# Two of the first layer's down products, for the second token half, and the first norm as work of the delta rule mixer's own order

## The chip, the cores and the metric

The kernel runs on one core of one Trainium2 chip. TensorE (PE) multiplies matrices into PSUM; VectorE (DVE), ScalarE (ACT) and GpSimd (POOL) do elementwise work; SyncE's queue (SP) issues nearly all transfers. The metric is the device time of one execution in microseconds (us), the median of several runs.

## What is computed

A trunk of two layers over 1024 tokens of width 1024, in float32. Layer 0 mixes tokens by gated linear attention, layer 1 by the gated delta rule; behind each mixer stands a dense feed-forward block, and a norm stands at the end:

```python
for i in range(DEPTH):
    hn = rms_norm(h, mix_norm_w[i])
    h = h + (gla_mixer(hn, ...) if i % 2 == 0 else gdn_mixer(hn, ...))
    h = h + swiglu(rms_norm(h, ffn_norm_w[i]), ffn_w_gate_up[i], ffn_w_down[i])
return rms_norm(h, final_norm_w)

def swiglu(h, w_gate_up, w_down):
    gate, up = jnp.split(h @ w_gate_up, 2, axis=-1)
    return (jax.nn.silu(gate) * up) @ w_down
```

What is changed is the last product of layer 0 (activations of 1024 x 2816 times `w_down`, 2816 x 1024, added to `h`) and the beginning of `gdn_mixer` in layer 1.

## The kernel before

Every large product keeps float32 accuracy with three matmuls: each operand is split into a rounded part `hi` (a cast on ACT) and the rest `lo` (a subtraction), and `hi*hi`, `hi*lo` and `lo*hi` are added in PSUM. The residual `h` stays on chip as 8 token tiles of 128 rows; a token half is 4 of them.

**The down products (`downs`).** The product is cut 2 x 2 x 2 (tokens in halves, 2816 in even and odd k-tiles, 1024 columns in halves) and computed by seven products of sums instead of eight. Each of the seven runs over 11 k-tiles in 6 groups (one of 1, five of 2) with 4 token tiles: 132 matmuls of 128x512. Three loops hold two products each in step, a fourth holds one; PSUM banks `pa` collect four of the products and are added to a place of `h` after each, `pc` is used for the other three. The activations come from DRAM (`act`), the weights from the input; loads and sums go through tiles `ra*`, `rb*` of two buffers, the sums `sk`, `tk` stay. Operands are split by ACT and DVE into three slots per tag.

**The mixer (`gdn`).** It opens its own pools: `wraw` (tag `raw`, two slots) for what is loaded, `wsplit` (tags `whi` and `wlo`, two slots each) for the split, made by `loadw` with ACT for `whi` and POOL for `wlo`. The first norm (`norm(0)`) runs ahead of everything, then a written-out order: strands (`seq`, `post`, `join`, `prep`, `inputs`, `solve`, one unit after another, 16 units) go on whenever their event or due time on a virtual clock has come, and `dense` (projections `keys`, `values`, `late`, and the output product `out`) fills PE in between. PE keeps this order; the other engines and SP are ordered by a planner that simulates. A unit's `solve` is a chain of 31 steps of two DVE instructions, with transfers before and after it; `join`, `seq` and `post` follow. `values(1)` waits until `seq(0)` has turned its values, `keys(3)` until `seq(0)` has passed, `values(2)` for `seq(1)`. The part of the code that stands at the mixer's start is:

```python
for _ in norm(0):
    pass
with self.tc.manual_schedule(engines={mybir.EngineType.PE}):
    O.run([each(seq), each(post), each(join), each(prep), inputs(), each(solve)], dense())
```

`addout` multiplies two k-tiles of an output product for each token tile and adds the result to `h` on DVE. `lowproj` is the narrow projection that the gates need; it takes slots of `raw` and `whi` as well.

Of the kernel before, what the change touches and what calls it, by code (L numbers as in the profile page):

```python
# [22 lines left out]
P = 128  # L23
D = 1024
# [71 lines left out]
class Trunk:  # L96
# [63 lines left out]
    def loadw(self, srcs, shape):  # L160

        nc = self.nc
        raw = self.wr.tile(shape, F32, name="raw", tag="raw")
        hi = self.ws.tile(shape, F32R, name="whi", tag="whi")
        lo = self.ws.tile(shape, F32R, name="wlo", tag="wlo")
        for sl, src in srcs:
            nc.sync.dma_start(raw[:, :, sl], src)
        nc.scalar.copy(hi, raw)  # L168

        n = shape[1] // 4 or 1  # L170
        for k in range(0, shape[1], n):
            sl = slice(k, k + n)
            if shape[2] * n > 256:
                for c in range(0, shape[2], 256):
                    cs = slice(c, c + 256)
                    nc.gpsimd.tensor_tensor(out=lo[:, sl, cs], in0=raw[:, sl, cs], in1=hi[:, sl, cs].bitcast(F32),  # L176
                                            op=ALU.subtract)
            else:
                nc.gpsimd.tensor_tensor(out=lo[:, sl], in0=raw[:, sl], in1=hi[:, sl].bitcast(F32), op=ALU.subtract)  # L179
        return hi, lo  # L180

    def loadcols(self, w, cols):

# [132 lines left out]

    def addout(self, half, w, lhs, cc):

        for t in range(C):
            ps = self.dps()  # L320
            for k in range(2):
                self.mm3(ps, [v[:, t * P:(t + 1) * P] for v in lhs[k]],
                         [v[:, k, :] for v in w], k == 0, k == 1)
                yield
            o = self.h[:, half * C + t, cc * 512:(cc + 1) * 512]
            self.nc.vector.tensor_tensor(out=o, in0=o, in1=ps, op=ALU.add)  # L326

    def loadrows(self, w, r0, cc):

# [9 lines left out]

    def outparts(self, half, w, r0, oT):  # L340
        for cc in range(2):
            yield from self.addout(half, self.loadrows(w, r0, cc), oT, cc)

    def outproj(self, *args):
        for _ in self.outparts(*args):
# [243 lines left out]
    def gdn(self):  # L589
# [5 lines left out]
        with ExitStack() as es:  # L595
# [22 lines left out]

            def gates(x, half):

                pl = self.lowproj(w_in, 6 * D, B, x)
                low = mx.tile([2 * B, HT], F32, name="low", tag="raw", bufs=2)
                S.copy(low, pl[0:2 * B, :])
                yield 2.0
# [49 lines left out]
            keyed, valued, scored, solved, joined, turned, passed, posted, gating = (events() for _ in range(9))  # L674
            gated = [Event(), Event()]
            gts = [None, None]
            U = [{} for _ in range(UN)]
            x = []

# [36 lines left out]
            def values(n):  # L716
                if n < UN:
                    if n:
                        yield turned[n - 1]
                    for i in range(2):  # L720
                        yield from conv(16 + 2 * (n % NQ) + i, f"v{i}", n, valued if i else None)
# [22 lines left out]

            def inputs():

                yield from gates(x, 0)
                yield free[1]
                yield from norm(1)
                O.set(ready[1], 1.0)  # L750
                yield from gates(x, 1)
                yield free[2]
                yield from self.normparts(self.head, 0, self.ffnw[1], self.xp, mx, "raw")
                O.set(ready[2], 1.0)

            def dense():
                yield from keys(0)
                yield from values(0)
                yield from late(0)
                yield from keys(1)  # L760
                yield from late(1)
                yield from keys(2)
                yield from values(1)
                for m in range(1, UN):
                    if m + 2 in (NQ, UN):
                        yield from values(m + 1)
                        yield from late(m + 1)
                        O.set(free[1 if m + 2 == NQ else 2])
                        yield from out(m - 1)
                        if m + 2 == NQ:  # L770
                            yield ready[1]
                            yield from keys(NQ)
                    else:
                        yield from keys(m + 2)
                        yield from out(m - 1)
                        yield from values(m + 1)
                        yield from late(m + 1)
                yield ready[2]
                yield from self.headparts(1, mx, ("v", "v", "raw"))
                yield from out(UN - 1)  # L780
# [276 lines left out]
            def each(f):  # L1057
                for n in range(UN):
                    yield from f(n)
            for _ in norm(0):  # L1060
                pass
            with self.tc.manual_schedule(engines={mybir.EngineType.PE}):
                O.run([each(seq), each(post), each(join), each(prep), inputs(), each(solve)], dense())

# [46 lines left out]
    def ffn(self, l):  # L1111
        with ExitStack() as es:
            xo = self.pool(es, "xops", 1)
            B = dict(b11=[t[:, 0:4] for t in self.head], b21=[t[:, 4:8] for t in self.head])
            for n in ("t1", "t2", "b22", "t3", "t4"):
                B[n] = [xo.tile([P, 4, HT], F32R, name=f"{n}{h}", tag=f"{n}{h}") for h in ("hi", "lo")]
            self.inputsums(l, B)
            self.gateups(l, B)
        self.xs.__exit__(None, None, None)
        self.downs(self.a["ffn_w_down"][l], self.act)  # L1120

    def pool(self, es, name, bufs, **kw):
        return es.enter_context(self.tc.tile_pool(name=name, bufs=bufs, reuse_waits="tile", **kw))
# [124 lines left out]
                V.tensor_tensor(out=p1, in0=p1, in1=pa, op=ALU.mult)  # L1248
                nc.sync.dma_start(self.act[f][:, 0:HT], p1)

    def downs(self, w, act):

# [5 lines left out]
        with ExitStack() as es:  # L1260
# [26 lines left out]
            def product(g, x, y, pss, first, outs):  # L1287
# [3 lines left out]
                for t in range(C):  # L1291
                    self.prod(pss[t], [v[:, :, t * P:(t + 1) * P] for v in x], y, first and g[0] == 0)
                    if g is groups[-1]:
                        for th, ch in outs:
                            o = self.h[:, th * C + t, ch * HT:(ch + 1) * HT]
                            V.tensor_tensor(out=o, in0=o, in1=pss[t], op=ALU.add)

            banks = lambda own: [own() for _ in range(3)] + [self.prepps()]
            of = lambda t, g: t[:, g[0]:g[0] + g[1]]
            pa, pc = banks(self.dps), banks(self.seqps)  # L1300
            for g in groups:
                b11, a11 = b(g, 0, 0), a(g, 0, 0)
                product(g, a11, b11, pa, True, [(0, 0)])
                b12, a21, a22 = b(g, 0, 1), a(g, 0, 1), a(g, 1, 1)
                s1, t1 = of(sk, g), of(tk, g)
                sum_(s1, a21, a22, ALU.add)
                sum_(t1, b12, b11)
                product(g, s1, t1, pc, True, [(1, 1), (0, 1)])
            pc = banks(self.seqps)
            for g in groups:  # L1310

                a11, b22 = a(g, 0, 0), b(g, 1, 1)
                s, t = of(sk, g), of(tk, g)
                sum_(s, s, a11)
                sum_(t, b22, t)
                product(g, s, t, pa, False, [(0, 1)])
                a12, b21 = a(g, 1, 0), b(g, 1, 0)
                product(g, a12, b21, pc, True, [(0, 0)])
                sum_(s, a12, s)
            pc = banks(self.seqps)  # L1320
            for g in groups:
                a11, a21, b12, b22 = a(g, 0, 0), a(g, 0, 1), b(g, 0, 1), b(g, 1, 1)
                sum_(a11, a11, a21)
                sum_(b12, b22, b12)
                product(g, a11, b12, pa, False, [(1, 1)])
                product(g, of(sk, g), b22, pc, True, [(0, 1)])
# [87 lines left out]
```

## Time and profile before

| | us |
|---|---|
| median of 3 runs | 3215.63 (3211.54 to 3217.33) |
| profiled execution | 3215.21 |
| its span, first to last instruction | 3213.4 |
| mean granted TensorE clock | 0.965 |
| down products of layer 0, PE | 1031.1 to 1243.5 |
| first projection of the mixer | 1261.83 |

Times inside the profile count from the span's first instruction. Busy times of engines overlap. A matmul's duration includes its way through the array; what counts for a row of matmuls is the distance between their starts.

### The profile page before, as it was taken

How to read it: one execution, taken by the hardware profiler on the slowest of the kernel's cores; microseconds unless marked ns; L12 is line 12 of the kernel's file. 1: busy time of each engine (PE TensorE's matmuls, PEld its weight loads, DVE VectorE, ACT ScalarE, POOL GpSimd, SP SyncE). 2: the span in 40 equal slices, each digit the busy share in tenths (PEclk: the TensorE clock that was granted, in tenths of full speed). 3: DMA queues.
4: the chain of work that ended last, by engine and by line, in shares of the span. 5: the costliest groups of instructions: out<-in, count | busy, mean ns of one | idle time of the engine just before them, and what ended most of it. 6: DMA issues, size and time to landing. Idle time of an engine off the chain costs nothing.

```text
span 3213.4 us, 41887 instructions
## 1 busy us (share of the span) xinstructions
PE 2948.6 (92%) x14547; PEld 2433.6 (76%) x14547; DVE 1968.8 (61%) x4228; ACT 1410.4 (44%) x2581; POOL 1300.5 (40%) x1561
## 2 busy tenths in 40 slices
PE   6999999899999998879999987999999889999998
PEld 5877777678887887667777776777777668888786
DVE  5364665633223875777777868778778543332786
ACT  5354454433433334435444453554544433333333
POOL 5454654545553002613443444344444445555001
PEclk9999999999999999889999998999999899999999
DMA  4222222332223842312222212222232232221862
GB/s 127 73 61 66 66 61 69 94 106 79 89 82 115 287 144 67 86 32 72 70 73 66 66 54 72 61 71 71 65 79 63 86 112 79 86 79 60 293 221 92
DMA packets 386882, 296.83 MB, mean 92 GB/s; under 512 B 70087, under 2 KB 312206, under 8 KB 386670
## 3 DMA queue, kind: packets, MB, share of 16 engines
q1 hardware_dynamic: 386606, 294.15, 30.4%
q8 instruction: 114, 1.87, 0.2%
q14 instruction: 98, 0.80, 0.1%
q0 software_dynamic: 64, 0.02, 0.0%
HBM read 259.49 MB, written 34.60 MB: 92 GB/s over the span
## 4 chain that ended last, share of the span: by engine, by line
PE 64%; DVE 24%; DMA 4%; issue 3%; ACT 3%; POOL 2%; SPq 1%; DVEq 0%; POOLq 0%; ACTq 0%
PE pd L211 38%; PE pq L211 14%; PE pp L211 8%; DVE xix L896 4%; DVE tmpx L894 4%; DVE v L702 1%; DMA nbx<-d 1%; POOL wlo L179 1%; PE pp L494 1%; DVE k L702 1%; DVE h L326 1%; PE pp L217 1%; DMA rb<-in_ffn_w_down_dram 1%; DVE st L496 1%; DMA p<-part 1%
## 5 line engine op out<-in xcount | busy, mean ns | idle before, releaser
L179 POOL TENSOR_TENSOR wlo<-raw,whi 128x256 fp32r<-128x256 f32 x624 | 473.9, 789 | 463.5 <-ACT whi L168 424.4
L211 PE MATMUL pd<-xhi,whi 128*128 128x512 f32 x1072 | 448.0, 418 | 0.8 <-ACT part L1093 0.7
L211 PE MATMUL pd<-xhi,wlo 128*128 128x512 f32 x1072 | 426.1, 397 | 0.0
L211 PE MATMUL pd<-xlo,whi 128*128 128x512 f32 x1072 | 424.9, 396 | 0.0
L168 ACT CAST whi<-raw 128x1024 fp32r<-128x1024 f32 x204 | 213.8, 1049 | 247.2 <-PE pd L211 140.7
L1129 POOL TENSOR_TENSOR olo<-s,ohi 128x512 fp32r<-128x512 f32 x152 | 195.9, 1290 | 205.9 <-ACT ohi L1128 205.9
L1129 POOL TENSOR_TENSOR olo<-raw,ohi 128x512 fp32r<-128x512 f32 x138 | 190.8, 1385 | 202.8 <-ACT ohi L1128 178.3
L211 PEld LDWEIGHTS pd<-xhi,wlo 128*128 128x128 f32 x1072 | 204.4, 191 | 46.1 <-POOL wlo L179 0.5
L176 POOL TENSOR_TENSOR wlo<-raw,whi 128x256 fp32r<-128x256 f32 x192 | 146.5, 792 | 217.9 <-ACT whi L168 200.0
L211 PEld LDWEIGHTS pd<-xhi,whi 128*128 128x128 f32 x1072 | 205.3, 192 | 38.4 <-ACT part L1093 1.7
L211 PEld LDWEIGHTS pd<-xlo,whi 128*128 128x128 f32 x1072 | 205.6, 192 | 36.7 <-issue 0.3
L1128 ACT CAST ohi<-s 128x512 fp32r<-128x512 f32 x152 | 94.3, 622 | 230.6 <-PE pd L211 174.0
L211 PE MATMUL pd<-whi,ohi 128*128 128x512 f32 x384 | 165.9, 432 | 11.9 <-ACT q L700 8.7
L894 DVE TENSOR_TENSOR tmpx<-nbx,xix 128x60 f32<-128x60 f32 (+24 forms) x496 | 152.0, 307 | 35.9 <-DMA nbx<-d 23.2
L1128 ACT CAST ohi<-raw 128x512 fp32r<-128x512 f32 x138 | 85.1, 620 | 198.1 <-POOL olo L1129 177.5
L896 DVE TENSOR_TENSOR xix<-xix,tmpx 128x60 f32<-128x60 f32 (+24 forms) x496 | 161.1, 325 | 13.0
L326 DVE TENSOR_TENSOR h<-h,pd 128x512 f32<-128x512 f32 x192 | 130.4, 683 | 53.5 <-PE pd L211 52.9
L211 PE MATMUL pd<-wlo,ohi 128*128 128x512 f32 x384 | 156.3, 407 | 1.6 <-POOL wlo L176 1.6
L211 PE MATMUL pd<-whi,olo 128*128 128x512 f32 x384 | 154.3, 402 | 0.0
L1237 DVE TENSOR_TENSOR p<-p,pp 128x512 f32<-128x512 f32 x38 | 26.1, 688 | 197.9 <-DMA raw<-in_ffn_w_gate_up_dram 143.4
L211 PE MATMUL pd<-bhi,ahi 128*128 128x512 f32 x264 | 104.4, 396 | 13.9 <-ACT ahi L1283 13.9
L1283 ACT CAST ahi<-ra 128x1024 fp32r<-128x1024 f32 (+1 forms) x48 | 47.1, 981 | 131.3 <-PE pp L211 78.0
(396 smaller groups left out, 7892.7 us busy)
## 6 DMA issues: line engine op xcount, KB each, us to landing
raw<-in_gdn_w_in_dram SPq DMA_DIRECT2D x96, 512.0 KB, 4.0
raw<-in_ffn_w_gate_up_dram SPq DMA_DIRECT2D x176, 256.0 KB, 3.2
ra<-act SPq DMA_DIRECT2D x176, 256.0 KB, 5.8
rb<-in_ffn_w_down_dram SPq DMA_DIRECT2D x70, 512.0 KB, 6.4
raw<-in_gla_w_in_dram SPq DMA_DIRECT2D x48, 512.0 KB, 3.8
raw<-in_gdn_w_out_dram SPq DMA_DIRECT2D x32, 512.0 KB, 3.9
act<-p SPq DMA_DIRECT2D x44, 256.0 KB, 2.0
act<-u SPq DMA_DIRECT2D x38, 256.0 KB, 2.0
```

The costliest lines, as they stand in the source:

```text
L168: nc.scalar.copy(hi, raw)
L176: nc.gpsimd.tensor_tensor(out=lo[:, sl, cs], in0=raw[:, sl, cs], in1=hi[:, sl, cs].bitcast(F32), op=ALU.subtract)
L179: nc.gpsimd.tensor_tensor(out=lo[:, sl], in0=raw[:, sl], in1=hi[:, sl].bitcast(F32), op=ALU.subtract)
L211: self.nc.tensor.matmul(out, lhsT, rhs, start=start, stop=stop, **kw)
L217: self.nc.tensor.transpose(ps[:, c * P:(c + 1) * P], src(c), self.ident)
L326: self.nc.vector.tensor_tensor(out=o, in0=o, in1=ps, op=ALU.add)
L702: V.scalar_tensor_tensor(out=out, in0=raw[:, s:s + HT], scalar=tap(s), in1=out, op0=ALU.mult, op1=ALU.add)
L894: V.tensor_tensor(out=tv, in0=nbx[:, s, s + 1:].unsqueeze(2).to_broadcast([P, m, w]), in1=xv[:, s:s + 1, 0:w].to_broadcast([P, m, w]), op= ...
L896: V.tensor_tensor(out=xv[:, s + 1:, 0:w], in0=xv[:, s + 1:, 0:w], in1=tv, op=ALU.add)
L1128: self.nc.scalar.copy(hi, src)
L1129: eng.tensor_tensor(out=lo, in0=src, in1=hi.bitcast(F32), op=ALU.subtract)
L1283: S.copy(hi, src)
```

## The change

In layer 0 (`later`), `downs` no longer computes the product of (a11 - a21) and (b22 - b12), which belongs to both column halves of the second token half, nor the one of a22 and t4, which belongs to its first columns. It writes three of the sums to DRAM tiles (`spill`) and keeps a list of tiles in `self.rest`; the content of `pa` after the second loop is added to three places of `h` instead of one. In the mixer, `dense` begins with the first of the two products (`restparts(0)`), then waits for `norm(0)`, which is now the first thing of the strand `inputs`, computes `lowproj` and goes on as before; `restparts(1)` stands between `keys(2)` and `values(1)`. `restparts` loads two k-tiles of x and of w, splits both with `splitw` and calls `addout`, which adds each pair of k-tiles to `h`. The last layer's downs are unchanged.

```diff
--- before.py
+++ after.py
@@ -165,6 +165,12 @@
         lo = self.ws.tile(shape, F32R, name="wlo", tag="wlo")
         for sl, src in srcs:
             nc.sync.dma_start(raw[:, :, sl], src)
+        self.splitw(raw, hi, lo)
+        return hi, lo
+
+    def splitw(self, raw, hi, lo):
+        nc = self.nc
+        shape = raw.shape
         nc.scalar.copy(hi, raw)
 
         n = shape[1] // 4 or 1
@@ -177,7 +183,6 @@
                                             op=ALU.subtract)
             else:
                 nc.gpsimd.tensor_tensor(out=lo[:, sl], in0=raw[:, sl], in1=hi[:, sl].bitcast(F32), op=ALU.subtract)
-        return hi, lo
 
     def loadcols(self, w, cols):
 
@@ -316,14 +321,16 @@
 
     def addout(self, half, w, lhs, cc):
 
+        n = len(lhs)
         for t in range(C):
             ps = self.dps()
-            for k in range(2):
+            for k in range(n):
                 self.mm3(ps, [v[:, t * P:(t + 1) * P] for v in lhs[k]],
-                         [v[:, k, :] for v in w], k == 0, k == 1)
+                         [v[:, k, :] for v in w], k == 0, k == n - 1)
                 yield
-            o = self.h[:, half * C + t, cc * 512:(cc + 1) * 512]
-            self.nc.vector.tensor_tensor(out=o, in0=o, in1=ps, op=ALU.add)
+            for c in cc:
+                o = self.h[:, half * C + t, c * 512:(c + 1) * 512]
+                self.nc.vector.tensor_tensor(out=o, in0=o, in1=ps, op=ALU.add)
 
     def loadrows(self, w, r0, cc):
 
@@ -339,7 +346,7 @@
 
     def outparts(self, half, w, r0, oT):
         for cc in range(2):
-            yield from self.addout(half, self.loadrows(w, r0, cc), oT, cc)
+            yield from self.addout(half, self.loadrows(w, r0, cc), oT, [cc])
 
     def outproj(self, *args):
         for _ in self.outparts(*args):
@@ -618,7 +625,11 @@
 
             def gates(x, half):
 
-                pl = self.lowproj(w_in, 6 * D, B, x)
+                if half:
+                    lows.append(self.lowproj(w_in, 6 * D, B, x))
+                else:
+                    yield lowed
+                pl = lows[half]
                 low = mx.tile([2 * B, HT], F32, name="low", tag="raw", bufs=2)
                 S.copy(low, pl[0:2 * B, :])
                 yield 2.0
@@ -674,6 +685,7 @@
             keyed, valued, scored, solved, joined, turned, passed, posted, gating = (events() for _ in range(9))
             gated = [Event(), Event()]
             gts = [None, None]
+            lows, lowed = [], Event()
             U = [{} for _ in range(UN)]
             x = []
 
@@ -744,6 +756,8 @@
 
             def inputs():
 
+                yield from norm(0)
+                O.set(ready[0], 1.0)
                 yield from gates(x, 0)
                 yield free[1]
                 yield from norm(1)
@@ -754,12 +768,17 @@
                 O.set(ready[2], 1.0)
 
             def dense():
+                yield from self.restparts(0)
+                yield ready[0]
+                lows.append(self.lowproj(w_in, 6 * D, B, x))
+                O.set(lowed)
                 yield from keys(0)
                 yield from values(0)
                 yield from late(0)
                 yield from keys(1)
                 yield from late(1)
                 yield from keys(2)
+                yield from self.restparts(1)
                 yield from values(1)
                 for m in range(1, UN):
                     if m + 2 in (NQ, UN):
@@ -1057,8 +1076,6 @@
             def each(f):
                 for n in range(UN):
                     yield from f(n)
-            for _ in norm(0):
-                pass
             with self.tc.manual_schedule(engines={mybir.EngineType.PE}):
                 O.run([each(seq), each(post), each(join), each(prep), inputs(), each(solve)], dense())
 
@@ -1117,7 +1134,7 @@
             self.inputsums(l, B)
             self.gateups(l, B)
         self.xs.__exit__(None, None, None)
-        self.downs(self.a["ffn_w_down"][l], self.act)
+        self.downs(self.a["ffn_w_down"][l], self.act, later=l == 0)
 
     def pool(self, es, name, bufs, **kw):
         return es.enter_context(self.tc.tile_pool(name=name, bufs=bufs, reuse_waits="tile", **kw))
@@ -1248,7 +1265,24 @@
                 V.tensor_tensor(out=p1, in0=p1, in1=pa, op=ALU.mult)
                 nc.sync.dma_start(self.act[f][:, 0:HT], p1)
 
-    def downs(self, w, act):
+    def restparts(self, i):
+
+        xs, ws, cc = self.rest[i]
+        for at in range(0, len(xs), 2):
+            kp = min(2, len(xs) - at)
+            full = slice(0, HT)
+            parts = []
+            for ts in (xs, ws):
+                raw = self.wr.tile([P, 2, HT], F32, name="raw", tag="raw")[:, 0:kp]
+                hi, lo = (self.ws.tile([P, 2, HT], F32R, name=n, tag=n)[:, 0:kp] for n in ("whi", "wlo"))
+                for k in range(kp):
+                    self.nc.sync.dma_start(raw[:, k, :], ts[at + k])
+                self.splitw(raw, hi, lo)
+                parts.append((hi, lo))
+            x, w = parts
+            yield from self.addout(1, w, [[v[:, k, :] for v in x] for k in range(kp)], cc)
+
+    def downs(self, w, act, later):
 
 
 
@@ -1295,6 +1329,12 @@
                             o = self.h[:, th * C + t, ch * HT:(ch + 1) * HT]
                             V.tensor_tensor(out=o, in0=o, in1=pss[t], op=ALU.add)
 
+            def spill(nm, g, src):
+                for i in range(g[1]):
+                    d = self.kept[nm, g[0] + i] = self.dr.tile([P, HT], F32, name=f"{nm}{g[0] + i}", tag=f"{nm}{g[0] + i}")
+                    nc.sync.dma_start(d, src[:, i])
+
+            self.kept = {}
             banks = lambda own: [own() for _ in range(3)] + [self.prepps()]
             of = lambda t, g: t[:, g[0]:g[0] + g[1]]
             pa, pc = banks(self.dps), banks(self.seqps)
@@ -1306,6 +1346,9 @@
                 sum_(s1, a21, a22, ALU.add)
                 sum_(t1, b12, b11)
                 product(g, s1, t1, pc, True, [(1, 1), (0, 1)])
+                if later:
+                    sum_(a11, a11, a21)
+                    spill("s3", g, a11)
             pc = banks(self.seqps)
             for g in groups:
 
@@ -1313,11 +1356,24 @@
                 s, t = of(sk, g), of(tk, g)
                 sum_(s, s, a11)
                 sum_(t, b22, t)
-                product(g, s, t, pa, False, [(0, 1)])
+                product(g, s, t, pa, False, [(0, 1), (1, 0), (1, 1)] if later else [(0, 1)])
                 a12, b21 = a(g, 1, 0), b(g, 1, 0)
                 product(g, a12, b21, pc, True, [(0, 0)])
                 sum_(s, a12, s)
+                if later:
+                    sum_(t, b21, t)
+                    spill("t4", g, t)
             pc = banks(self.seqps)
+            if later:
+                for g in groups:
+                    b12, b22 = b(g, 0, 1), b(g, 1, 1)
+                    product(g, of(sk, g), b22, pc, True, [(0, 1)])
+                    sum_(b12, b22, b12)
+                    spill("t3", g, b12)
+                tiles = lambda nm: [self.kept[nm, i] for i in range(n)]
+                self.rest = ((tiles("s3"), tiles("t3"), (0, 1)),
+                             ([act[2 * i + 1][:, HT:T] for i in range(n)], tiles("t4"), (0,)))
+                return
             for g in groups:
                 a11, a21, b12, b22 = a(g, 0, 0), a(g, 0, 1), b(g, 0, 1), b(g, 1, 1)
                 sum_(a11, a11, a21)
```

## Rows read from the trace of the kernel before

**Rows 1.** The page: span, and busy time of each engine.

```profile
span 3213.4 us, 41887 instructions
PE 2948.6 (92%) x14547; PEld 2433.6 (76%) x14547; DVE 1968.8 (61%) x4228; ACT 1410.4 (44%) x2581; POOL 1300.5 (40%) x1561
```

**Rows 2.** Windows table: start:end, length, busy (count) per engine, clock, DMA share, GB/s.

```profile
1031.10:1243.50 212.40, 212.34 (x924) 175.00 (x924) 160.57 (x164) 80.13 (x86) 7.05 (x18) 0.99 0.61 206
1243.50:1261.80 18.30, 10.38 (x49) 6.61 (x49) 13.87 (x32) 8.40 (x16) 4.70 (x5) 0.81 0.00 0
1261.80:1340.50 78.70, 76.94 (x361) 62.58 (x359) 55.26 (x133) 42.15 (x59) 49.20 (x74) 1.00 0.34 89
1340.50:1374.30 33.80, 21.37 (x123) 18.29 (x123) 21.41 (x62) 14.18 (x20) 10.46 (x19) 0.70 0.19 43
1374.30:1389.10 14.80, 14.80 (x74) 12.17 (x72) 13.50 (x48) 6.89 (x18) 4.32 (x10) 1.00 0.16 43
1389.10:1423.50 34.40, 15.48 (x69) 12.93 (x69) 22.91 (x82) 11.19 (x32) 5.46 (x12) 0.60 0.16 40
```

**Rows 3.** Timeline of PE, downs to mixer: start, duration, instruction, [idle before <-releaser].

```profile
1243.22 0.39 PE L211 MATMUL pp<-bhi,alo 128*128 128x512 f32 x1
1250.43 0.45 PE L217 MATMUL pp<-cst,xn 128*128 128x128 f32 x1 [6.82 <-issue]
...
1261.83 0.39 PE L211 MATMUL pd<-xhi,whi 128*128 128x512 f32 x1
```

**Rows 4.** Timeline of PE, the two holes behind `keys(2)`.

```profile
1374.25 0.48 PE L211 MATMUL pd<-xhi,whi 128*128 128x512 f32 x1
...
1412.93 0.55 PE L211 MATMUL pq<-xd,nt 128*128 128x128 f32 x1 [11.19 <-DVE tmpx L894]
...
1423.50 0.48 PE L211 MATMUL pd<-xhi,whi 128*128 128x512 f32 x1
```

**Rows 5.** The chain of waits in the downs: start, length, what.

```profile
1143.47 5.09 DMA rb<-in_ffn_w_down_dram
1148.59 1.23 DVE tk L1279
...
1216.41 4.08 PE pd L211 x18
```

**Rows 6.** The page's costliest groups: `addout`'s additions to `h`.

```profile
L326 DVE TENSOR_TENSOR h<-h,pd 128x512 f32<-128x512 f32 x192 | 130.4, 683 | 53.5 <-PE pd L211 52.9
```

**Rows 7.** Timelines of ACT and POOL: splits in the mixer's start and projections.

```profile
1235.16 0.39 ACT L198 CAST w<-raw 128x256 fp32r<-128x256 f32 x1
1235.69 0.73 POOL L199 TENSOR_TENSOR w<-raw,w 128x256 fp32r<-128x256 f32 x1 [2.41 <-ACT w L198]
...
1268.54 1.06 ACT L168 CAST whi<-raw 128x1024 fp32r<-128x1024 f32 x1 [2.03 <-PE pd L211]
...
1306.38 2.80 POOL L179 TENSOR_TENSOR wlo<-raw,whi 128x256 fp32r<-128x256 f32 x4 [5.08 <-ACT whi L168]
```

**Rows 8.** Timeline of PE: a gap behind a split, and matmuls behind a gap.

```profile
659.85 0.79 PE L211 MATMUL pd<-xhi,olo 128*128 128x512 f32 x1 [4.40 <-POOL olo L1129]
...
1514.34 1.19 PE L211 MATMUL pq<-gstate,k 128*128 128x256 f32 x2 [3.57 <-DVE gstate L1014]
...
1516.61 0.63 PE L211 MATMUL pd<-xlo,whi 128*128 128x512 f32 x1
1517.04 0.63 PE L211 MATMUL pd<-xhi,wlo 128*128 128x512 f32 x1
...
1517.75 0.40 PE L211 MATMUL pd<-xlo,whi 128*128 128x512 f32 x1
```

**Rows 9.** Timelines of DVE (solve steps) and POOL (subtractions) at the same time.

```profile
1321.45 0.66 DVE L894 TENSOR_TENSOR tmpx<-nbx,xix 128x29 f32<-128x29 f32 x1
...
1323.75 0.22 DVE L894 TENSOR_TENSOR tmpx<-nbx,xix 128x54 f32<-128x54 f32 x1
...
1320.62 2.83 POOL L179 TENSOR_TENSOR wlo<-raw,whi 128x256 fp32r<-128x256 f32 x4 [0.43 <-ACT whi L168]
```

## Prediction

> **What bounds the kernel now.** The page comes first [rows 1]: TensorE (PE) is busy for 92% of the span, no other engine for more than 61%. Work that PE cannot drop is worth nothing; what can be won is PE's idle time. The windows table, cut at the borders of the stretches that the change touches, says where that lies [rows 2]. In the first layer's down products PE is busy for 212.34 of 212.40 us, 924 matmuls, no gap. Then it has little to do for 18.3 us (10.38 us of slow, short matmuls), until the mixer's first projection. The six projections `keys(0)` to `keys(2)` run nearly solid. Behind them are two thin stretches: 1340.5 to 1374.3 (21.37 of 33.8 us busy) and 1389.1 to 1423.5 (15.48 of 34.4). The PE timeline shows the edges [rows 3, 4]: last down matmul at 1243.22, first transpose at 1250.43, first projection at 1261.83; `values(1)` starts at 1374.25; `keys(3)` at 1423.50, after PE waited 11.19 us for the solve on VectorE (DVE). Idle in the two holes: 12.4 + 18.9 = 31.3 us.
>
> So the change moves two full-speed stretches of PE work from a place without gaps to places with gaps. The question is how well the moved work runs there.
>
> **Removed from the downs.** Two products are 2 x 11 k-tiles x 4 token tiles x 3 matmuls = 264 of the 924 [rows 2]. 18 take 4.08 us on the chain, 0.227 us each [rows 5]: **-59.9 us**. The last down matmul should then stand near 1183.5.
>
> **Added in the downs.** Three spills of 11 tiles each (33 writes of 256 KB) on SP's queue and two sums moved earlier; the number of sums is unchanged. At the end of the second loop DVE adds `pa` to three places, 12 adds where 4 stood: 8 x 0.683 = 5.5 us [rows 6]. Before, PE has slack there by a hair: the chain around 1143 runs through a late `rb` load and DVE's `tk` [rows 5], and each spill is one more issue in SP's order that loads stand behind. Nothing to all of this and a late load or two: 0 to 8; I take **+3**, since the three slots per operand tag let operands be made two products ahead.
>
> **The product behind the downs, restparts(0).** It needs 132 matmuls, 29.9 us. But its operands are split differently. In the downs there are three slots per operand tag; here `whi` and `wlo` come from a pool of two, and each group of two k-tiles takes both slots of each tag, one for x and one for w. A projection takes one slot, and even so its cast of the weights after next starts only when PE lets go of a slot (the ACT row with 2.03 us of waiting for PE [rows 7]). For restparts this means that nothing of group g+1 can be split before PE has finished group g. After the last matmul of a group stand: cast of x 1.06 us; four POOL subtractions for x, 2.80; two for the first half of w, 1.40 [rows 7]; about 0.4 of hand-overs (estimate): PE's second matmul comes 5.7 us later, and the second half of w is there after 7.1. Then some 20 matmuls, 4.5 us: 11.6 us a group instead of 5.4. The x and w loads hide behind this, since `raw` is freed by the split. The nearest gap of this kind in the trace is the 4.40 us in which PE waits for a POOL subtraction behind a cast [rows 8].
>
> Such gaps have a second price. After an idle 3.57 us, PE's matmuls run with 0.43 us between starts instead of 0.227, from 1514.34 to about 1517.5 [rows 8], at the 1.2 GHz level: 1.6 us lost. I charge that per full group and 1 us at the short one. Groups: 5.5 for the first, 4 x (11.6 + 1.6), and for the last, of one tile, 3.8 (half the chain) + 2.5 (11 matmuls) + 1.0: 65.6 us; with the norm's 32 transposes and four POOL multiplications in between, +4: **70 us**. From below, 58 (no clock loss, transposes in the gaps); 47 if there were no gaps at all, because then DVE sets the pace with 48 adds of 0.683 [rows 6] and 13.87 us for the norm [rows 2]; from above, 77.
>
> Behind it `lowproj` and the first `keys` weights also need slots that the last group holds: cast and subtraction of the narrow one 0.39 + 0.73, of the wide one 1.06 + 2.80 [rows 7], with hand-overs about **+5.5** (4 to 7). Before, the same border cost 18.3 us [rows 2]. Sum up to `keys(0)`: -59.9 + 3 + 70 + 5.5 - 18.3 = **+0.3 us**. All that was taken out of the downs is spent before the first projection.
>
> **The product in the hole, restparts(1).** From 1340.5 to 1423.5 are 83 us with 51.7 busy [rows 2]: 14.8 of `values(1)` and about 37 of unit work, some of it at half clock (granted 0.70 and 0.60), so about 28 at full speed. Into that come 65.6 us of groups and 3.5 for the first one, one of whose slots `keys(2)` still holds: 14.8 + 28 + 69 = 112, +29, if no gap between groups is used by unit work. PE's order is written beforehand as if a group took 5.4 us, so units stand within groups as often as between them: with half of the 27 us of gaps filled, 98, **+15**. The lower bound is 0 (everything lies in the 31.3 us and in the gaps). DVE's 24 further adds (16 us) and POOL's 44 subtractions lie beside this. What is late next: `values(1)`, the first unit's recurrence, and with it `keys(3)`.
>
> Sum: +0.3 + 15 = +15 against the profiled execution's 3215.21, which is 0.4 under the median of the runs: **3230 us**. A difference of 6.4 us (0.2%) is about what a measurement here can tell from none.
>
> **Rivals.** *Faster: the gaps cost nothing where PE was idle anyway.* If the holes swallow restparts(1) whole and restparts(0) takes its lower 58 us, the sum is -59.9 + 1 + 58 + 4.5 - 18.3 = -15, 3200; without gaps at all, -26, 3190. It decides when restparts(0) stays under about 63 us and `keys(3)` starts no more than 83 us after `keys(2)` ends. For it speak the 31.3 idle us [rows 2] and the 11.19 us wait, which more dense work can cover [rows 4]; against it the slots. The Trainium skill, Perfetto Trace Analysis, Optimization Strategy, says that interleaving regimes with different most-contended engines may help; the down products and the mixer's start are such a pair, and by it this rival holds. Chance 0.24.
>
> *Same: the two parts cancel,* restparts(1) mostly hidden, 3209 to 3222. Chance 0.16.
>
> *Slower still: POOL's subtractions hold up the solve.* While four `wlo` subtractions run on POOL (2.83 us), a small solve step on DVE takes 0.66 us; just after, one of nearly twice the elements takes 0.22 [rows 9]. restparts(1) brings 44 such subtractions, 31 us, into the time of solve(0)'s end and solve(1), which is 62 steps. If half of that falls on the solve at two thirds lost, it ends 10 us later, and `join(1)`, `values(2)` with it: 15 + 10 and up to the +29 bound, 3240 to 3258. The Trainium skill, SBUF — State Buffer, Who interferes with whom, has this as a rule: a VectorE instruction with two SBUF inputs contends with a GpSimd instruction that reads SBUF. Against it: solve(1) has waited for its turn before anyway. Chance 0.15.
>
> **How the numbers follow.** Forecast (slower by 6.4 to 24 us) 0.45, slower still 0.15, same 0.16, faster 0.24. Slower 0.60, same 0.16, faster 0.24. The range leaves out the gapless case and half of the rest of the faster one below (about 0.12), and the upper end of the port rival (about 0.07): 3202 to 3247. The likeliest case alone: 3222 to 3239.
>
> **What would show it.** Right: last down matmul at 1184 to 1190; then, in restparts(0), gaps of 5 to 6 us on PE every 11 to 14 us, ended by ACT `whi` or POOL `wlo`, and half-speed matmuls behind them; first projection at 1255 to 1270; the same gaps behind `keys(2)`; `keys(3)` some 98 us behind its end. Wrong: gaps under 2 us (the splits do run ahead), or the holes' waits gone with `keys(3)` as soon after `keys(2)` as before, or down matmuls with new waits for loads that end past 1195.

## The result and the profile after

The changed kernel takes 3265.16 us (median of 4 runs, 3261.77 to 3268.83) against 3213.59 of the kernel before: ratio 1.0161, 95% interval 1.0148 to 1.0174. Slower, as forecast, but by 51.6 us where 14.8 were forecast, and outside the range. Its profiled execution took 3268.07 us. The page [rows 1]:

```profile
span 3266.3 us, 42135 instructions
PE 2974.2 (91%) x14547; PEld 2442.4 (75%) x14547; DVE 2002.3 (61%) x4276; ACT 1408.7 (43%) x2581; POOL 1361.5 (42%) x1649
```

PE has as many matmuls as before. The windows table of the changed kernel, cut at the same borders as [rows 2], with the columns given there:

```profile
1029.20:1187.00 157.80, 154.30 (x661) 125.73 (x661) 135.30 (x140) 57.87 (x60) 4.94 (x8) 0.98 0.76 258
1187.00:1269.50 82.50, 55.16 (x181) 38.03 (x180) 44.68 (x80) 20.14 (x30) 38.49 (x60) 0.73 0.25 72
1269.50:1347.80 78.30, 75.65 (x358) 62.02 (x356) 49.37 (x128) 42.30 (x59) 45.91 (x73) 1.00 0.33 89
1347.80:1448.10 100.30, 62.87 (x260) 47.68 (x258) 64.59 (x154) 25.55 (x33) 42.27 (x69) 0.76 0.24 70
1448.10:1477.40 29.30, 24.51 (x143) 20.70 (x142) 21.34 (x61) 16.84 (x51) 10.01 (x19) 1.00 0.32 91
```

Row by row: the downs fell from 212.4 to 157.8 us. The border up to `keys(0)`, which now holds restparts(0), grew from 18.3 to 82.5, and the granted clock in it is 0.73. `keys(0)` to `keys(2)` are as they were (78.7, now 78.3). From there to `keys(3)` it takes 129.6 us, the last two rows, where 83.0 stood. The sum, -54.6 + 64.2 - 0.4 + 46.6 = +55.8, holds the whole difference of the spans (+52.9); some 3 us are given back outside these stretches, 2 of them ahead of the downs, where the code is the same.

How restparts(0) runs, on PE's timeline, where its second group begins:

```profile
1194.67 0.39 PE L216 MATMUL pd<-whi,wlo 128*128 128x512 f32 x1
1196.96 0.49 PE L216 MATMUL pd<-whi 128*128 128x512 f32 x1 [1.90 <-ACT whi L174]
1200.30 0.80 PE L216 MATMUL pd<-wlo,whi 128*128 128x512 f32 x1 [2.84 <-POOL wlo L182]
1200.89 0.63 PE L216 MATMUL pd<-whi,wlo 128*128 128x512 f32 x1
1201.32 0.63 PE L216 MATMUL pd<-whi 128*128 128x512 f32 x1
```

PE waits for the cast, does one matmul, waits for the subtractions, and then starts matmuls 0.43 us apart, at the 1.2 GHz level, where 0.227 was usual [rows 5]. The groups of PE's instructions in this stretch add it up (line, engine, operation | busy, mean ns | idle before, what ended it):

```profile
L216 PE MATMUL pd<-wlo,whi 128*128 128x512 f32 x44 | 22.9, 520 | 14.5 <-POOL wlo L182 14.5
L216 PE MATMUL pd<-whi 128*128 128x512 f32 x44 | 22.6, 514 | 9.3 <-ACT whi L174 9.3
L222 PE MATMUL pp<-cst,xn 128*128 128x128 f32 x32 | 6.4, 336 | 2.5 <-issue 2.5
```

That is 23.8 us of waiting for splits. The hole behind `keys(2)` has more of it, the same groups from 1347.8 to 1448.1:

```profile
L216 PE MATMUL pd<-wlo,whi 128*128 128x512 f32 x44 | 23.6, 536 | 16.0 <-POOL wlo L182 16.0
L216 PE MATMUL pd<-whi 128*128 128x512 f32 x44 | 22.9, 520 | 21.3 <-ACT whi L174 18.5 <-DVE h L333 2.9
```

The edges of that stretch on PE's timeline [rows 4]:

```profile
1358.44 0.79 PE L216 MATMUL pd<-whi 128*128 128x512 f32 x1 [10.29 <-ACT whi L174]
...
1428.72 1.05 PE L216 MATMUL pq<-xd,nt 128*128 128x128 f32 x8
...
1448.08 0.48 PE L216 MATMUL pd<-xhi,whi 128*128 128x512 f32 x1
...
1467.96 1.06 PE L216 MATMUL pq<-xd,nt 128*128 128x128 f32 x8
...
1477.38 0.48 PE L216 MATMUL pd<-xhi,whi 128*128 128x512 f32 x1
```

The first group waits 10.29 us for its cast. ACT's timeline tells why:

```profile
1343.37 0.69 ACT L712 ACTIVATE k<-pd,col_conv 128x512 f32<-128x512 f32 x1
1353.85 0.63 ACT L716 ACTIVATE k<-k 128x512 f32<-128x512 f32 x1 [9.79 <-DVE k L714]
...
1357.34 1.05 ACT L174 CAST whi<-raw 128x1024 fp32r<-128x1024 f32 x1
```

The cast stands in ACT's order behind the convolution of unit 2's k, which waits 9.79 us for DVE, and DVE is in solve(0), whose last step ends at 1357.08. `join(0)`'s first matmul starts at 1428.72, although its operand `xd` had left DVE at 1373.96 (1372.72 + 1.24 on DVE's timeline): in PE's written order four whole groups and most of a fifth stand ahead of it. Then `values(1)` at 1448.08 and `keys(3)` at 1477.38.

### The profile page after: what moved, and what is told of

It reads as the page before. It is cut to its first block, busy times and chain, and to the rows that moved or that the text cites. A ratio compares the mean times of both kernels' runs of the same rounds, so it can differ in the third digit from the quotient of the medians.

```text
span 3266.3 us, 42135 instructions
## 1 busy us (share of the span) xinstructions
PE 2974.2 (91%) x14547; PEld 2442.4 (75%) x14547; DVE 2002.3 (61%) x4276; ACT 1408.7 (43%) x2581; POOL 1361.5 (42%) x1649
## 5 line engine op out<-in xcount | busy, mean ns | idle before, releaser
L185 POOL TENSOR_TENSOR wlo<-raw,whi 128x256 fp32r<-128x256 f32 x624 | 476.5, 793 | 471.4 <-ACT whi L174 436.7
L182 POOL TENSOR_TENSOR wlo<-raw,whi 128x256 fp32r<-128x256 f32 x280 | 208.9, 776 | 420.8 <-ACT whi L174 217.0
L174 ACT CAST whi<-raw 128x1024 fp32r<-128x1024 f32 (+1 forms) x228 | 236.4, 1041 | 318.2 <-PE pd L216 195.0
L333 DVE TENSOR_TENSOR h<-h,pd 128x512 f32<-128x512 f32 x264 | 177.6, 683 | 95.3 <-PE pd L216 94.7
L913 DVE TENSOR_TENSOR tmpx<-nbx,xix 128x60 f32<-128x60 f32 (+24 forms) x496 | 156.5, 316 | 54.5 <-DMA nbx<-d 41.2
L1418 POOL TENSOR_TENSOR y<-y,fw 128x512 f32<-128x512 f32 x6 | 8.8, 1483 | 221.9 <-ACT y L1417 221.9
L1259 DVE TENSOR_TENSOR u<-u,pq 128x512 f32<-128x512 f32 x38 | 26.1, 688 | 115.7 <-PE pq L216 115.7
```

The costliest lines, as they stand in the source:

```text
L913: V.tensor_tensor(out=tv, in0=nbx[:, s, s + 1:].unsqueeze(2).to_broadcast([P, m, w]), in1=xv[:, s:s + 1, 0:w].to_broadcast([P, m, w]), op= ...
L1259: V.tensor_tensor(out=u2, in0=u2, in1=pc, op=ALU.add)
```

## Experiments

Two ideas could explain the size. **Slots:** every group takes both slots of `whi` and `wlo`, so split and multiplication alternate, and the idle time brings half-speed matmuls. **Place:** PE's written order, made with 5.4 us a group, puts the first unit's join behind groups that take 14. Rivals to both: POOL's own rate or its port, something in the norm's move, or the two products hurting one another.

All times are medians, and each ratio is to the kernel before as measured beside that run. The stretches are read from PE's timeline: the downs from the start of their first matmul to the end of their last, the border from there to the start of `keys(0)`, and from that start to the start of `keys(3)`.

| kernel | us | ratio, interval | downs | border | to keys(3) |
|---|---|---|---|---|---|
| before | 3213.6 | | 212.5 | 18.2 | 161.7 |
| changed | 3265.2 | 1.0161 (1.0148-1.0174) | 157.8 | 82.5 | 207.8 |
| norm alone | 3220.1 | 1.0021 (1.0012-1.0031) | 211.6 | 22.1 | 163.6 |
| first product and norm | 3252.0 | 1.0125 (1.0110-1.0141) | 190.1 | 77.9 | 162.3 |
| second product and norm | 3230.6 | 1.0052 (1.0035-1.0068) | 182.2 | 21.2 | 210.3 |
| four slots | 3232.0 | 1.0067 (1.0048-1.0085) | 158.9 | 54.4 | 207.7 |
| planned | 3249.4 | 1.0118 (1.0101-1.0135) | 159.2 | 80.9 | 195.6 |
| four slots but first, planned | 3225.8 | 1.0043 (1.0026-1.0059) | 159.0 | 57.6 | 197.9 |
| the same, hole split | 3223.9 | 1.0037 (1.0024-1.0050) | 160.3 | 58.0 | 205.0 |
| half groups | 3226.8 | 1.0044 (1.0029-1.0059) | 159.8 | 69.4 | 180.6 |
| second product, old norm | 3220.4 | 1.0019 (1.0010-1.0028) | 182.5 | 18.1 | 204.4 |
| **the same in half groups** | **3198.8** | **0.9951 (0.9937-0.9965)** | 182.5 | 18.4 | 178.4 |
| the same, planned | 3203.2 | 0.9967 (0.9955-0.9980) | 182.0 | 18.6 | 189.8 |
| four slots and half groups | 3213.4 | 1.0000 (0.9991-1.0009) | 159.7 | 55.1 | 179.6 |

### One part of the change at a time

**The first product**, `restparts(0)` alone; the t4 product stays last in the downs, in banks of its own:

```diff
-                yield from self.restparts(1)
...
+                pa = banks(self.dps)
+                for g in groups:
...
+                    product(g, a22, t4, pa, True, [(1, 0)])
```

> Only the product s3 x t3 is moved (restparts(0)); the product with t4 stays in the downs, with banks of its own. If each move costs what the traces show for it by itself: the downs get 30 us back against the changed kernel (keys(0) near 1300, 7.7 + 30 us later than before) and the hole after keys(2) is as before (83 us to keys(3)), so about 3250 us. If the two moves hurt one another (the shared pools, the queue of loads), this one alone is much cheaper: 3220 to 3230.

**The second product**, `restparts(1)` alone; s3 x t3 stays in the third loop of the downs:

```diff
-                yield from self.restparts(0)
...
+                    product(g, a11, b12, pa, False, [(1, 1), (1, 0)])
```

> Only the product with t4 is moved (restparts(1)); s3 x t3 stays in the downs. By the traces the downs lose 30 us and the hole grows by 46.6 us: about 3230 us, keys(2) to keys(3) near 130 us. If the hole is only long because restparts(0) left the queues late, it falls back towards the predicted 98 us and the kernel ends near 3198.

**Neither**, only the norm and `lowproj` in the order:

```diff
-        self.downs(self.a["ffn_w_down"][l], self.act, later=l == 0)
+        self.downs(self.a["ffn_w_down"][l], self.act, later=False)
...
-                yield from self.restparts(0)
...
-                yield from self.restparts(1)
```

> No product is moved: the downs are those of before, and only the first norm and the low projection of the gates are work of the mixer's own order. The account so far (each moved product costs its own place, the norm's move nothing) expects 3210 to 3218 us. If the norm in the order is a cost by itself (its transposes and the low projection come later on PE than in the loop ahead of the order), it expects 3222 us or more.

Measured: 3252.0, 3230.6 and 3220.1. The parts add up: the norm's move +7 (3220.1 against 3212.8 measured beside it), the first product another +32, the second +11, together 50 of the 51.6. So the products do not hurt one another, and the hole is as long without restparts(0) (210.3) as with it. But the norm was not free: 3220.1 lies between the two expectations, above the one that gave it nothing. Its groups on PE, from the last down matmul to `keys(0)`:

```profile
L222 PE MATMUL pp<-cst,xn 128*128 128x128 f32 x32 | 7.8, 424 | 9.1 <-issue 6.7 <-DVE xlo L278 2.4
L208 PE MATMUL pd<-xhi,w 128*64 128x512 f32 x8 | 4.2, 527 | 0.0
```

Before, the low projection's matmuls stood between the transposes; now all 16 stand behind the last of them, the transposes wait for DVE instead (2.4 us), and the border takes 22.1 us in place of 18.2. That is about half of the 7; the next stretch is 1.9 us longer, and in the profiles the rest stands behind `keys(3)`; it was not traced.

### The slots

**Four slots in restparts(0):** w gets raw, hi and lo tiles from tags that nothing uses yet, so two groups can be held.

```diff
             for ts in (xs, ws):
+                if i == 0 and ts is ws:
+                    new = lambda p, dt, tag: p.tile([P, 2, HT], dt, name=tag, tag=tag, bufs=2)[:, 0:kp]
+                    raw, hi, lo = new(self.mx, F32, "at"), new(self.tp, F32R, "sz"), new(self.mx, F32R, "nt")
+                else:
...
+            self.mx = mx
```

> Both products moved, but in restparts(0) the w operand takes raw, hi and lo tiles of its own (two more slots of each, from tags that are idle then), so that a group's loads no longer wait for the group before it. If the two slots make the gaps: restparts(0) falls from 76 us to about 40 us (30 us of matmuls, 31 us of POOL's subtractions, the first group's ramp), its matmuls stay at full clock, and the kernel ends near 3230 us. If POOL's rate or its port shared with VectorE sets the pace, it stays above 65 us and the kernel above 3255 us. The hole after keys(2) is unchanged under both (130 us).

Measured 3232.0: the number of the slots' account, though restparts(0) itself takes 50 us (1184.6 to 1234.9) where about 40 were expected. The border falls from 82.5 to 54.4 us, and 10 of these are a wait ahead of the first group (w's load was issued only 3.5 us after the last down matmul, at 1188.1 on SP's queue). Window and PE's groups:

```profile
1184.60:1238.90 54.30, 40.98 (x180) 30.42 (x181) 44.66 (x80) 20.27 (x30) 38.00 (x60) 0.91 0.34 101
```

```profile
L216 PE MATMUL pd<-sz,whi 128*128 128x512 f32 x44 | 19.0, 432 | 10.4 <-ACT sz L174 10.0 <-DVE h L333 0.5
L216 PE MATMUL pd<-nt,whi 128*128 128x512 f32 x44 | 18.3, 415 | 0.8 <-POOL nt L182 0.8
```

The waits between groups are gone, with POOL's work unchanged (38.0 us, 38.5 in the changed kernel). So neither POOL's rate nor its port set the pace there. PE's busy time falls from 55.2 to 41.0 us for the same matmuls and the clock rises from 0.73 to 0.91: of the 28 us won, 14 are waits (with the new 10 us counted against them) and 14 are slow matmuls. Not all matmuls are at full clock, as was expected: behind that wait they start 0.43 us apart for the first 4 us.

**Half groups:** x and w of one 128-row step share a raw, hi and lo tile, in both places.

```diff
+        for at in range(len(xs)):
+            raw = self.wr.tile([P, 2, HT], F32, name="raw", tag="raw")
+            hi, lo = (self.ws.tile([P, 2, HT], F32R, name=n, tag=n) for n in ("whi", "wlo"))
...
+            self.splitw(raw, hi, lo)
+            yield from self.addout(1, [hi[:, 1:2], lo[:, 1:2]], [[hi[:, 0], lo[:, 0]]], cc)
```

> The changed kernel, with the groups of both products cut in two: the x and the w of one 128-row step share one raw, hi and lo tile, so the same two slots hold two groups and one is split while the other is multiplied. POOL's and ACT's work is the same, VectorE's adds into h double (92 to 132 more of 0.68 us over both products are hidden only where VectorE is idle). If the slots make the gaps in both places: restparts(0) near 48 us in place of 76, restparts(1) near 60 in place of 84, the kernel at 3205 to 3220 us. If in the hole the pace is set by the units' own work on VectorE, ACT and POOL, only restparts(0) shortens and the kernel ends at 3235 to 3245 us.

Measured 3226.8, between the two: the hole gains fully (207.8 to 180.6 to `keys(3)`), the border less than expected (82.5 to 69.4). DVE's groups in the border say why:

```profile
L333 DVE TENSOR_TENSOR h<-h,pd 128x512 f32<-128x512 f32 x88 | 54.5, 683 | 0.0
```

88 additions, without idle time ahead of them, 54.5 of 69.4 us, and with the norm's work DVE is busy for 66.3 of them: each half group adds into both column halves of `h`. (Over both products there are 132 additions where 72 stood, 60 more and not the 92 to 132 of the expectation.) With two columns the doubled adds become the bound; in the hole, where a group adds into one, there are half as many.

### The place

**Planned:** a group of restparts(1) is ready for the planner only 8 us after its loads are issued.

```diff
             x, w = parts
+            if i:
+                yield 8.0
             yield from self.addout(1, w, [[v[:, k, :] for v in x] for k in range(kp)], cc)
```

> The changed kernel, but each group of restparts(1) tells the planner that it is ready only 8 us later (about what its loads take), so PE's written order puts the first unit's join and what follows between the groups and not behind them. If the place of join(0) in PE's order is what makes the hole grow: join(0)'s first matmul comes near 1385 in place of 1428.7 and keys(2) to keys(3) falls to 95 to 110 us, the kernel to 3230 to 3245 us. If the slots alone set the hole (84 us of restparts(1) however they are mixed), it stays within 5 us of 130 us.

Measured 3249.4, 12 us less in the stretch. The join moved as expected, `keys(3)` only from 207.8 to 195.6 us behind `keys(0)`:

```profile
1382.83 1.39 PE L216 MATMUL pq<-xd,nt 128*128 128x128 f32 x11
...
1464.07 0.39 PE L216 MATMUL pd<-xhi,whi 128*128 128x512 f32 x1
```

PE's waits for splits fall all the same, from 34.5 to 7.9 us between `keys(2)` and `keys(3)`, but part of this comes back as waits of the units' own work for ACT and DVE (idle time 42.2 to 27.7 us). So place is a cause, but for a quarter of the hole's growth; `values(1)` still stands behind the last group.

**Four slots, but the first group in the ordinary tiles, and planned;** and **the same with restparts(1) cut in two** around `values(1)`:

```diff
-                if i == 0 and ts is ws:
+                if i == 0 and at and ts is ws:
```

```diff
-                yield from self.restparts(1)
+                yield from self.restparts(1, 0, 3)
                 yield from values(1)
+                yield from self.restparts(1, 3)
```

> The extra tiles for restparts(0) and the later ready times for restparts(1) together, and the first group of restparts(0) takes the ordinary tiles, which the downs do not hold, so that the 10 us wait ahead of it goes. If the two places add up: 3232 - 16 - 8 = 3208 us (3203 to 3213), a little faster than the kernel before. If the 10 us belonged to something else (the first loads, whatever tile they go to), 3216.

> As the kernel before it in this call, and restparts(1) is cut in two: three groups ahead of values(1), three behind it. In the planned kernel the first unit's v transposes end at 1400 and values(1) could start, but starts at 1450 behind the last groups. If PE's order is still the loss: values(1) starts near 1405 - 30 us, keys(3) comes 10 to 20 us earlier and the kernel ends at 3188 to 3200 us. If the groups cost the same wherever they stand (their own 14 us period), it ends within 4 us of the kernel with the groups together.

Measured 3225.8 and 3223.9: the first missed both of its numbers, the second came out by its other account, within 4 us of the groups together. In the first, the hole kept its gain (207.7 to 197.9), but the border did not: the 10 us ahead of group 0 went, but group 0 takes both ordinary slots again, and the waits came back at group 1 and behind it (PE's groups in the border):

```profile
L216 PE MATMUL pd<-sz,whi 128*128 128x512 f32 x36 | 16.9, 468 | 5.0 <-ACT whi L174 4.6 <-DVE h L333 0.4
L216 PE MATMUL pd<-sz,wlo 128*128 128x512 f32 x36 | 15.9, 440 | 2.5 <-POOL wlo L182 2.5
L222 PE MATMUL pp<-cst,xn 128*128 128x128 f32 x32 | 5.0, 280 | 4.1 <-DVE xn L299 3.9 <-POOL xn L299 0.2
```

In the second, `values(1)` came as wanted, 139.2 us behind `keys(0)` where it stands at 184.0 without the cut, but `keys(3)` came later (205.0 against 197.9 us) and the kernel is no faster: the groups cost the same behind `values(1)`. The place of `values(1)` is not a loss of its own.

### What beats both kernels

By the table, moving the second product is worth some 30 us in the downs (211.6 to 182.2) and costs 46 in the hole, but only some 17 to 19 with half groups; the first product's move costs in these stretches some 10 us more than it brings even with four slots (border 21.2 to 54.4, downs 182.2 to 158.9; in the medians, 3230.6 and 3232.0, that difference does not show); the norm's move costs 7. So: **the second product alone, with the norm ahead of the order** as before the change, in ordinary groups; **in half groups**; **in half groups and planned** (4 us); and, for comparison, **both products, four slots and half groups**, norm in the order.

```diff
-                yield from norm(0)
-                O.set(ready[0], 1.0)
...
-                yield from self.restparts(0)
-                yield ready[0]
-                lows.append(self.lowproj(w_in, 6 * D, B, x))
-                O.set(lowed)
...
+            for _ in norm(0):
+                pass
```

> Only the product with t4 is moved, in groups of two steps as in the changed kernel, and the first norm and the low projection stand ahead of the order as in the kernel before. If the norm's move costs its 7 us whatever else moves: 3230.6 - 7 = 3223 us. If the 7 us belong only to the kernel with no product moved, 3230.

> As the one with the old norm, but the product with t4 goes in groups of one step that share their tiles (x and w of a step in one), so that the two slots hold two groups. With both products moved, these half groups shortened the stretch from keys(0) to keys(3) from 207.8 to 180.6 us; if that carries over, 3223 - 27 = 3196 us (3192 to 3202), faster than the kernel before by 0.4 to 0.6%. If it was restparts(0) that gained by something else, and the hole's own pace is VectorE's (63 of 71 us busy there), about 3215.

> The same with half groups, and each is ready for the planner 4 us later, so that the first unit's join stands further ahead in PE's order. If place and slots are two separate losses: another 8 to 12 us, 3184 to 3190 us. If the half groups already bring the join early enough (its first product came 55 us after keys(2) with them, 81 us without), there is nothing more in it: within 3 us of the kernel without the planned times, or slower, as values(1) then starts behind more groups.

> Both products moved and the norm in the order, as in the change, with each mended: restparts(0) with tiles of its own for w, restparts(1) in half groups. If the two mends add up: 3232 - 27 = 3205 us (3200 to 3210). If the kernel is later held elsewhere: 3215 or more.

Measured 3220.4, **3198.8**, 3203.2 and 3213.4. The norm put back is worth 10 us (3230.6 to 3220.4). The half groups are worth another 21.6: faster than the kernel before, by 0.49% (interval 0.35 to 0.63). PE's groups between the last matmul of `keys(2)` and `values(1)`, first in ordinary groups (97.9 us), then in half groups (70.0 us):

```profile
L216 PE MATMUL pd<-wlo,whi 128*128 128x512 f32 x44 | 22.6, 513 | 16.6 <-POOL wlo L182 16.6
L216 PE MATMUL pd<-whi 128*128 128x512 f32 x44 | 21.7, 493 | 21.2 <-ACT whi L174 18.2 <-DVE h L333 3.0
```

```profile
L216 PE MATMUL pd<-whi 128*128 128x512 f32 x44 | 20.2, 458 | 11.3 <-DVE h L333 9.9 <-ACT whi L174 0.9 <-DVE rs_t L260 0.3
L216 PE MATMUL pd<-wlo,whi 128*128 128x512 f32 x44 | 19.3, 439 | 5.0 <-POOL wlo L182 5.0
```

Waiting for splits falls from 34.8 to 5.9 us. What is left is mostly one wait for an addition that stands in DVE's order behind solve(0):

```profile
1316.52 0.80 PE L216 MATMUL pd<-whi 128*128 128x512 f32 x1 [8.23 <-DVE h L333]
```

The place in PE's order is not the reason: 110 of the 131 matmuls of the product in this profile stand ahead of the first unit's join, and 111 of 132 with ordinary groups. The slots are what is left; ordinary groups with tiles of their own were not tried in the hole. The planned times on top bring nothing (4 us slower, the intervals overlap): the join now waits for DVE, not for PE's order, as its row there shows:

```profile
L216 PE MATMUL pq<-xd,nt 128*128 128x128 f32 x32 | 5.9, 352 | 13.0 <-DVE xd L926 13.0
```

So place was a loss only while the groups were long. The last kernel, both moves mended, equals the kernel before; 3205 was expected, or 3215 and more. Its border and hole are as in its two parents (55.1, 179.6), and their gains add up in these stretches. The missing 8 us lie outside them: against the four slots' profile 5.6 us stand behind `keys(3)` (1783.3 to 1788.9 us to the end) and 3.0 ahead of the downs, where the code is the same. Why the first of these arose stays open.

## Why the prediction was wrong

**Direction and mechanism were right.** The gaps came where they were forecast, ended by ACT `whi` and POOL `wlo`, with half-speed matmuls behind them, and four slots took them away. The faster rival, with its chance of 0.24, asked for restparts(0) under 63 us and an unchanged hole; both were missed.

**The downs:** -56.9 forecast, -54.6 measured; the last matmul ended at 1187.0, inside the forecast 1184 to 1190.

**The border was undersized by 7 us:** 75.5 forecast (70 + 5.5), 82.5 measured, just its bound of 77 + 5.5. The clock is the mis-sized term: 1.6 us a full group was charged, 7.4 in all, from one gap in [rows 8]; four slots gave back 14. The wait of 2.5 us ahead of the norm's first transposes was not in the sum either. The norm was priced at 4 us between the groups and 5.5 behind them, and the old border's 18.3 us were taken off in full; moved alone, it makes that border 22.1 and the kernel 7 us slower. How much of this is left when both products are moved, no run shows.

**The step that failed is the hole's.** It said "with half of the 27 us of gaps filled, 98, **+15**"; `keys(3)` came 129.6 us behind the end of `keys(2)`, +46.6, past even the bound of 112 that assumed no filling. Three things were wrong in it. No unit work filled the gaps: the groups behind the first waited 22.6 us for their splits (34.5 less the first group's 10.29 and 1.63), and what units put within the groups stands between matmuls that were ready. PE's idle time from `keys(2)` to `keys(3)` is 42.2 us (129.6 less 62.87 and 24.51), where the bound of 112 held 30.5 (27 + 3.5); PE's busy time, 87.4 us, is 6 more than that bound's (estimate: 14.8 + 28 + 69 - 30.5), with the clock at 0.76 up to `values(1)`. The first group's wait was priced by its slot at 3.5 us and was 10.29, because the cast stood in ACT's order behind a convolution that waited for DVE. And the join does not merely stand within a group: it stands behind four of them, at 1428.72, and `values(1)` behind the last; bringing it forward alone gave 12 of the 46.6, half groups in its place 27, and with half groups bringing it forward gave nothing more.

**The port rival (0.15)** came nearest in its time, 3240 to 3258, for a reason that the trace does not bear out. Single solve steps beside POOL's subtractions do take 0.65 instead of 0.19 us, first in the changed kernel, then in the one before (DVE's timelines, and the subtractions on POOL's):

```profile
1401.44 5.54 POOL L182 TENSOR_TENSOR wlo<-raw,whi 128x256 fp32r<-128x256 f32 x8 [7.64 <-ACT whi L174]
...
1400.97 0.18 DVE L913 TENSOR_TENSOR tmpx<-nbx,xix 128x31 f32<-128x31 f32 x1
...
1402.28 0.65 DVE L913 TENSOR_TENSOR tmpx<-nbx,xix 128x29 f32<-128x29 f32 x1
...
1427.10 0.17 DVE L915 TENSOR_TENSOR xix<-xix,tmpx 128x8 f32<-128x8 f32 x1
```

```profile
1376.09 0.18 DVE L894 TENSOR_TENSOR tmpx<-nbx,xix 128x31 f32<-128x31 f32 x1
...
1377.24 0.19 DVE L894 TENSOR_TENSOR tmpx<-nbx,xix 128x29 f32<-128x29 f32 x1
...
1403.77 0.17 DVE L896 TENSOR_TENSOR xix<-xix,tmpx 128x8 f32<-128x8 f32 x1
```

This is as in [rows 9]. The Trainium skill, SBUF — State Buffer, Who interferes with whom, says that a VectorE instruction with two SBUF inputs contends with a GpSimd instruction that reads SBUF; these rows agree. In solve(1) 16 of the 62 steps take over 0.55 us, where 6 did before. But solve(1) as a whole takes 26.3 us (to 1427.27) against 27.9 (to 1403.94), since less other work stands between its steps (3.4 us against 12.0), and it ends 41 us before PE's order comes to its join, at 1467.96, where PE has no wait.

**The pages.** The Trainium skill, Perfetto Trace Analysis, Optimization Strategy, says that interleaving regimes may help. With the change's groups it did not (1.0161); with half groups of one product it did (0.9951). The same section says that a gap repeating on the engine that should be saturated can mean too few buffers for the next tile; the four slots and the half groups agree.

## What to carry to other kernels

Work moved into a hole pays only if it can run at its old speed there: count the slots of the pool it will live in, and ask whether one group can be split while the last is multiplied. Halving a group so that two fit in the same slots cost no memory and turned +0.19% into -0.49%; it costs output additions, so it suits the product with one output. A planner that prices a step by its matmuls alone places it wrongly when the step has to wait, and in this kernel an idle gap was paid twice, since the matmuls behind it ran at the lower clock level.

## What the hardware showed that was not expected

The clock added half as much again to the waits. In the border of the changed kernel PE was busy for 55.2 us at a granted 0.73, with four slots 41.0 us at 0.91, for the same 180 matmuls and transposes: 14 us, beside 27 of idle time. Gaps of 1.9 and 2.8 us, one matmul apart, were followed by matmuls at the 1.2 GHz spacing of 0.43 us for 3 us or more, which is a quarter or more of each group behind the first, and nearly all of two of them.
